# State products four in a row into banks of two rings, and a contiguous tap table written in two bursts

## The chip, the cores and the metric

The kernel runs on one core of one Trainium2 chip, alone. The core has four engines that compute, which run at the same time and wait for one another by semaphores: TensorE (PE in the profile, with its weight loads as PEld), VectorE (DVE), ScalarE (ACT) and GpSimd (POOL). SyncE (SP) issues the transfers (DMA). SBUF is the working memory of 128 partitions, PSUM the memory with banks into which PE writes, DRAM the large one outside the core. The metric is the device time of one execution in microseconds (us).

## The reference

Two layers over 1024 frames of 1024 channels. Layer 0 is an RWKV-7 mixer, layer 1 a diagonal state-space mixer of 64 groups with 16 channels and 64 complex states each; after each stands an MLP of 4096, and every part ends in a norm, x <- LayerNorm(alpha * x + f(x)). The change touches the second mixer alone:

```python
def s5_mix(x, a_re, a_im, log_dt, b_re, b_im, c_re, c_im, d_skip, w_glu):
    ...
    def chunk_step(h, u_c):
        h_re, h_im = h
        bu_re = jnp.einsum('tbgc,gpc->tbgp', u_c, bbar_re)
        bu_im = jnp.einsum('tbgc,gpc->tbgp', u_c, bbar_im)
        pr, pi, sr, si = lax.associative_scan(combine, (a_ch_re, a_ch_im, bu_re, bu_im), axis=0)
        carry_re, carry_im = cmul(pr, pi, h_re[None], h_im[None])
        s_re = sr + carry_re
        s_im = si + carry_im
        y = (jnp.einsum('tbgp,gcp->tbgc', s_re, cr_w)
             - jnp.einsum('tbgp,gcp->tbgc', s_im, ci_w))
        return (s_re[-1], s_im[-1]), y
    ...
    y = y.transpose(2, 0, 1, 3, 4).reshape(bsz, seq, d) + xf * d_skip.astype(f32)
    y = jax.nn.gelu(y).astype(x.dtype)
    z = y @ w_glu
    return z[..., :d] * jax.nn.sigmoid(z[..., d:])
```

## The kernel before

The 1024 frames are worked on as two halves A and B of 512, channels on the partitions, in eight blocks of 128 channels. While one half is in a mixer, the other runs its MLP, so that PE has dense work beside the mixer's small steps. A scheduler orders the instructions of each engine: each has a due number (`rank` sets it for a part), and of what is ready the lowest goes first. Tables have 99500, the state-space layer 99300 (half A) and 99400 (half B), norms 99000.

**Dense products.** A weight block of 128x512 comes by SP into `wraw` (2 buffers, L169), ACT casts it to `whi` (L148), DVE subtracts to get `wlo` (L149; 3 buffers each), and PE does three products for each pair of high and low parts into `d` (L188). A block is 12 matmuls.

**Tables** (`s5_tables`, about 1070 to 1270 us of the profile). For each block f of 8 groups: `bc` is loaded, DVE and POOL expand it to `ca` and `bp` (L1110 to L1138), `ca` goes to the table tC in DRAM. PE makes the taps `pk` (L1151): the answer of a group to an input 0 to 7 frames back, for 16 channels, the even groups of a pair on partitions 0 to 15, the odd ones on 64 to 79 ("par"). ACT copies them into `kpad` (L1155), whose front half was cleared once by POOL (L1106), so that shifted windows of it read zeros. Two transfers (L1159, one for each par) write eight shifted windows of it as the tap table tT[f], with the group g as the innermost axis. kpad has one buffer, so the next block's copy waits until both have been read. Then `bs` goes to tB (L1168).

**State-space stage** (`s5`, once for A and once for B). The inputs are turned to sub-chunks of 8 frames: `u1`, `ug`. L1206 makes the input to each chunk's state from `tb`, DVE and POOL run the scan over 64 chunks in `hb`. Then the outputs, in four turns f2 of two blocks each: the tables `tt` (from tT, L1240) and `tcm` (from tC, L1242) come in four buffers that they share with `tb`; for each par in turn PE sums in one bank of the ring pc (2 banks) the tap products (L1250, 128 contracted rows, 64 columns of `ug` as weights, 128 moving columns of `tt`) and the state products (L1255, 64 contracted rows). With j the block of the pair, the two j write the two halves of the bank's partitions. ACT copies the bank to `y1` (L1257). PE turns y1 block by block into `pyt` (L1263, a bank of the ring pa, 2 banks), DVE adds the skip term (`yg`, one buffer), ACT does the Gelu (L1267) and SP stores `s_y` (L1268); `yl` reads it back for the GLU that follows.

A 64x64 product takes one quadrant of PE's array. The order between taps and states within a turn is the scheduler's. The norms use the ring pl (one bank, "l"), `d` a ring of 3.

Of the kernel before, what the change touches and what calls it, by code (L numbers as in the profile page):

```python
# [30 lines left out]
LNG = (1, 3, 5)  # L31
LNT = (2, 5)
TB = 2
LN8R = 400000
MIXR = 100
W0B = 5
# [34 lines left out]
def trunk(ctx, tc, A):  # L71
# [90 lines left out]
    def wload(src, kt, n, key=None):  # L162

        step = 512 // n
        out = []
        for k0 in range(0, kt, step):
            kept = low.get((key, k0)) if key else None
            raw = wp.tile([128, step, n], F32, tag="wraw", name="wraw", bufs=2)
            SP.dma_start(raw, src[:, k0 : k0 + step])  # L169
# [12 lines left out]
        return out  # L182

    bulk, hops = [], []
    ST = getattr(nc, STE)
# [833 lines left out]

    SL = 8  # L1020
    NSC = HT // SL
    tT = dr.tile([KT, 128, 2, 512], F32, name="tT")
    tB = dr.tile([KT, 128, 4, 2, 128], F32, name="tB")
    tC = dr.tile([KT, 128, 4, 2, 128], F32, name="tC")

    def s5_tables():
# [75 lines left out]
        V.tensor_sub(ci, ci, tq)  # L1102
        V.tensor_mul(ci, ci, den)

        kpad = pp.tile([128, 16, 16, 4], F32, name="kpad")
        G.memset(kpad, 0.0)  # L1106
        for f in range(KT):
            gs = slice(4 * f, 4 * f + 4)
            bc = pp.tile([128, 2, 2, 4, 16], F32, tag="bc", name="bc", bufs=1)
            SP.dma_start(bc, A["s5bc"][f])  # L1110
            bb = pp.tile([128, 2, 4, 16], F32, tag="bb", name="bb", bufs=1)
# [40 lines left out]
                                  ca[ps_, g2, ri, 0:8].rearrange("p t c -> p (t c)"), start=ri == 0, stop=ri == 1)  # L1152
            for par in range(2):
                ps_ = slice(64 * par, 64 * par + 16)
                S.copy(kpad[ps_, 8:].rearrange("p t c g -> p g (t c)"), p[ps_])  # L1155
            tv = tT[f].rearrange("(s c) two n -> two c s n", c=16)
            for par in range(2):
                src = kpad[64 * par : 64 * par + 16, 1:9].rearrange("p t c g -> p (t c g)")
                SP.dma_start(tv[par], bass.AP(src.tensor, src.offset, [src.ap[0], (64, SL), src.ap[1]]))  # L1159

            bs = pp.tile([128, 4, 2, 128], F32, tag="bs", name="bs", bufs=1)
            for hf in range(2):
# [10 lines left out]
    def s5(H, h):  # L1173
# [61 lines left out]
        for f2 in range(4):  # L1235
            y1 = s5p.tile([128, SL, 4, 2, 16], F32, tag="u1", name="y1", bufs=2)
            tabs = []
            for f in (2 * f2, 2 * f2 + 1):
                tt = s5p.tile([128, 2, 512], F32, tag="tab", name="tt", bufs=4)
                SP.dma_start(tt, tT[f])  # L1240
                tcm = s5p.tile([128, 4, 2, 128], F32, tag="tab", name="tcm", bufs=4)
                SP.dma_start(tcm, tC[f])  # L1242
                tabs.append((f, tt.rearrange("p two (n g) -> p two g n", g=4), tcm))
            for par in range(2):
                qs = slice(64 * par, 64 * par + 64)
                p = pc.tile([128, HT], F32, tag="c", name="py").rearrange("p (g n) -> p g n", g=4)

                for g2 in range(4):
                    for j, (f, tv, tcm) in enumerate(tabs):
                        PE.matmul(p[64 * j : 64 * j + 64, g2], ug[f][:, 2 * g2 + par], tv[:, par, g2],  # L1250
                                  start=g2 == 0, stop=False, skip_group_check=True)
                for g2 in range(4):
                    for ri in range(2):
                        for j, (f, tv, tcm) in enumerate(tabs):
                            PE.matmul(p[64 * j : 64 * j + 64, g2], hb[qs, 4 * f + g2, ri, 0:NSC], tcm[qs, g2, ri],  # L1255
                                      start=False, stop=ri == 1, skip_group_check=True)
                S.copy(y1[:, :, :, par].rearrange("p t g c -> p g t c"), p.rearrange("p g (t c) -> p g t c", t=SL))  # L1257
            for j in range(2):
                f = 2 * f2 + j
                js = slice(64 * j, 64 * j + 64)  # L1260
                p = pa.tile([128, SL, NSC], F32, tag="a", name="pyt")
                for t in range(SL):
                    PE.transpose(p[:, t], y1[js, t].rearrange("p g r c -> p (g r c)"), ident[js, js])  # L1263
                y = s5p.tile([128, HT], F32, tag="yg", name="yg", bufs=1)
                V.scalar_tensor_tensor(y.rearrange("p (c t) -> p t c", t=SL), h[f].rearrange("p (c t) -> p t c", t=SL),
                                       vec("d", f), p, op0=ALU.mult, op1=ALU.add)
                S.activation(y, y, AF.Gelu_apprx_tanh)  # L1267
                SP.dma_start(scr["y"][f * 128 : (f + 1) * 128, H * HT : (H + 1) * HT], y)  # L1268
# [127 lines left out]
```

## Time and profile before

| | before |
|---|---|
| median of 3 runs | 2742.12 us (2735.79 to 2742.68) |
| profiled execution, its own time | 2746.6 us |
| span in the profile | 2744.8 us |
| granted TensorE clock, mean | 0.961 |
| ACT busy | 1154.8 us (42%) |
| POOL busy | 630.6 us (23%) |
| DMA moved | 345.90 MB, mean 126 GB/s |

The profile is of one execution, and its span leaves out 1.8 us around it. In the rows below, "x" is a count; for a tile the view gives the shortest, median and longest duration in ns, then the first and last start. A row of a timeline is start, length, engine, line, operation, out<-in, shape and count, and in brackets the idle time before it and what ended it. A row of waits is the engine and its line, what it waited for, then the sum in us, the times, and the longest. "SPq" is SP's queue of transfers. An fp32 matmul leaves two records.

### The profile page before, as it was taken

The numbers are of one execution on the slowest core, as the hardware profiler recorded it, in microseconds if no ns is written. First come the engines' busy times: TensorE is split into PE (matmuls) and PEld (weight loads), VectorE is DVE, ScalarE is ACT, GpSimd is POOL, SyncE is SP. The second block draws the span as 40 slices with busy tenths as digits, with TensorE's granted clock in tenths as the row PEclk, the third lists the DMA queues.
The fourth block names the chain that finished last, engine by engine and source line by source line (L and its number), as shares of the span: only waits on it lengthen the run. The fifth ranks groups of instructions, "written<-read, shape, count | busy, mean of one in ns | idle before, by whom it ended". The sixth has DMA issues, their size and how long they took to land.

```text
span 2744.8 us, 43807 instructions
## 1 busy us (share of the span) xinstructions
PE 2598.4 (95%) x16582; PEld 2089.9 (76%) x16582; DVE 1813.3 (66%) x3191; ACT 1154.8 (42%) x2038; POOL 630.6 (23%) x515
## 2 busy tenths in 40 slices
PE   7999979989899999989999999999999999999997
PEld 5778757678677777767876788778778887788886
DVE  7477677577786867997567553674855546755556
ACT  7455574544543333353532332434223324433334
POOL 3121542432442122342122000120220101210101
PEclk9989979999899999999999999999999999999998
DMA  4765455564223334545333533233343322333333
GB/s 146 235 214 175 151 164 156 178 203 142 81 86 88 93 92 148 141 129 163 100 112 127 174 95 100 81 96 112 103 164 110 96 96 81 119 96 96 96 96 100
DMA packets 215058, 345.90 MB, mean 126 GB/s; under 512 B 21184, under 2 KB 75584, under 8 KB 214848
## 3 DMA queue, kind: packets, MB, share of 16 engines
q1 hardware_dynamic: 214848, 343.10, 40.5%
q8 instruction: 131, 2.15, 0.3%
q14 instruction: 79, 0.65, 0.1%
HBM read 279.06 MB, written 63.96 MB: 125 GB/s over the span
## 4 chain that ended last, share of the span: by engine, by line
PE 44%; DVE 4%; issue 3%; DMA 1%; POOL 1%; ACT 1%; ACTq 0%; SPq 0%; DVEq 0%; POOLq 0%
PE d L188 39%; PE py L1250 1%; PE py L1255 1%; DVE wlo L149 1%; DMA wraw<-in_mw_dram 1%; PE pu L154 1%; PE pbu L1206 1%; POOL rl L975 1%; DVE hA L991 0%; DMA s_y<-yg 0%; DVE t L1218 0%; DVE hB L991 0%; ACT whi L148 0%; DVE sq L876 0%; PE pu L1195 0%
## 5 line engine op out<-in xcount | busy, mean ns | idle before, releaser
L148 ACT CAST whi<-wraw 128x512 fp32r<-128x512 f32 x668 | 413.5, 620 | 929.1 <-PE d L188 623.2
L149 DVE TENSOR_TENSOR wlo<-wraw,whi 128x512 fp32r<-128x512 f32 x668 | 500.6, 750 | 426.8 <-ACT whi L148 404.3
L188 PE MATMUL d<-qbuf,whi 128*128 128x512 f32 (+1 forms) x2112 | 657.0, 394 | 23.8 <-DVE hA L991 12.8
L188 PEld LDWEIGHTS d<-qbuf,whi 128*128 128x128 f32 x2112 | 391.8, 191 | 120.0 <-DVE hA L991 17.8
L188 PE MATMUL d<-qbuf,wlo 128*128 128x512 f32 (+1 forms) x1056 | 411.9, 392 | 10.7 <-DVE wlo L149 10.4
L975 POOL TENSOR_TENSOR rl<-rl 128x512 f32<-128x512 f32 x128 | 157.2, 1228 | 1094.5 <-ACT rl L974 1094.5
L188 PE MATMUL d<-oAh,whi 128*128 128x512 f32 (+1 forms) x960 | 390.9, 411 | 15.5 <-ACT ev L418 6.3
L188 PE MATMUL d<-oAl,whi 128*128 128x512 f32 (+1 forms) x960 | 387.5, 405 | 3.0 <-DVE oAl L149 2.8
L188 PE MATMUL d<-oAh,wlo 128*128 128x512 f32 (+1 forms) x960 | 386.5, 405 | 2.4 <-DVE wlo L149 2.3
L188 PE MATMUL d<-oBh,whi 128*128 128x512 f32 x704 | 279.2, 397 | 0.0
L188 PE MATMUL d<-oBh,wlo 128*128 128x512 f32 x704 | 278.7, 396 | 0.2 <-DVE wlo L149 0.2
L188 PE MATMUL d<-oBl,whi 128*128 128x512 f32 x704 | 277.1, 394 | 0.0
L188 PEld LDWEIGHTS d<-qbuf,wlo 128*128 128x128 f32 x1056 | 201.7, 191 | 56.5 <-DVE wlo L149 14.5
L188 PEld LDWEIGHTS d<-oAh,whi 128*128 128x128 f32 (+1 forms) x960 | 185.9, 194 | 62.2 <-ACT ev L418 8.4
L188 PEld LDWEIGHTS d<-oAh,wlo 128*128 128x128 f32 (+1 forms) x960 | 185.8, 194 | 44.4 <-DVE wlo L149 3.2
L188 PEld LDWEIGHTS d<-oAl,whi 128*128 128x128 f32 (+1 forms) x960 | 185.6, 194 | 43.1 <-DVE oAl L149 5.2
L991 DVE TENSOR_TENSOR hB<-hB,d 128x512 f32<-128x512 f32 (+1 forms) x256 | 165.0, 650 | 71.2 <-PE d L188 68.0
L991 DVE TENSOR_TENSOR hA<-hA,d 128x512 f32<-128x512 f32 x240 | 162.1, 682 | 64.4 <-PE d L188 62.1
L188 PEld LDWEIGHTS d<-oBh,wlo 128*128 128x128 f32 x704 | 132.9, 189 | 32.4 <-issue 2.0
L188 PEld LDWEIGHTS d<-oBl,whi 128*128 128x128 f32 x704 | 133.1, 189 | 29.9 <-issue 0.7
L188 PEld LDWEIGHTS d<-oBh,whi 128*128 128x128 f32 x704 | 133.1, 189 | 29.0 <-issue 1.2
L149 DVE TENSOR_TENSOR qbuf<-rl,qbuf 128x512 fp32r<-128x512 f32 x128 | 95.0, 742 | 73.5 <-ACT qbuf L148 73.5
(374 smaller groups left out, 3804.8 us busy)
## 6 DMA issues: line engine op xcount, KB each, us to landing
wraw<-in_mw_dram SPq DMA_DIRECT2D x520, 256.0 KB, 2.7
wraw<-in_glu_dram SPq DMA_DIRECT2D x64, 256.0 KB, 2.7
low<-wlo SPq DMA_DIRECT2D x52, 256.0 KB, 2.6
wlo<-low SPq DMA_DIRECT2D x52, 256.0 KB, 3.6
wraw<-in_wk_dram SPq DMA_DIRECT2D x32, 256.0 KB, 3.5
wraw<-in_wr_dram SPq DMA_DIRECT2D x32, 256.0 KB, 3.9
wraw<-in_wv_dram SPq DMA_DIRECT2D x32, 256.0 KB, 4.3
yl<-s_y SPq DMA_DIRECT2D x32, 256.0 KB, 3.1
```

The lines of the kernel that those rows point to most:

```text
L148: S.copy(hi, src)
L149: (e or V).tensor_sub(lo, src, hi.bitcast(F32))
L154: PE.matmul(out, x, idt, start=True, stop=True)
L188: bulk.append((PE.matmul(p, w, x, **kw).ins, x.shape[-1]))
L975: G.tensor_mul(r, r, r)
L991: V.tensor_add(z, z, p)
L1206: PE.matmul(p[qs, g2, ri], tb[:, g2, ri, qs], u[:, 2 * g2 + par], start=True, stop=True)
L1250: PE.matmul(p[64 * j : 64 * j + 64, g2], ug[f][:, 2 * g2 + par], tv[:, par, g2], start=g2 == 0, stop=False, skip_group_check=True)
L1255: PE.matmul(p[64 * j : 64 * j + 64, g2], hb[qs, 4 * f + g2, ri, 0:NSC], tcm[qs, g2, ri], start=False, stop=ri == 1, skip_group_check=True)
```

## The change

The taps keep their values; the table's layout, the order of products and the banks change.

```diff
+    def inorder(prods):
+        for x, y in zip(prods, prods[1:]):
+            tc.add_manual_dep(y.ins, x.ins.name, mybir.DependencyInfo(
+                mybir.DependencyClass.NoSync, mybir.DependencyReason.DATA), reason="order")
...
-    tT = dr.tile([KT, 128, 2, 512], F32, name="tT")
+    tT = dr.tile([128, 2, KT, 4, 128], F32, name="tT")
...
-        kpad = pp.tile([128, 16, 16, 4], F32, name="kpad")
-        G.memset(kpad, 0.0)
+        kpads = [pp.tile([128, TBF, 4, 16, 16], F32, name=f"kpad{j}") for j in range(KT // TBF)]
+        for kpad in kpads:
+            G.memset(kpad[:, :, :, 0:8], 0.0)
         for f in range(KT):
+            kpad = kpads[f // TBF]
...
-                S.copy(kpad[ps_, 8:].rearrange("p t c g -> p g (t c)"), p[ps_])
-            tv = tT[f].rearrange("(s c) two n -> two c s n", c=16)
-            for par in range(2):
-                src = kpad[64 * par : 64 * par + 16, 1:9].rearrange("p t c g -> p (t c g)")
-                SP.dma_start(tv[par], bass.AP(src.tensor, src.offset, [src.ap[0], (64, SL), src.ap[1]]))
+                S.copy(kpad[ps_, f % TBF, :, 8:].rearrange("p g t c -> p g (t c)"), p[ps_])
+            if f % TBF == TBF - 1:
+                for par in range(2):
+                    for s in range(SL):
+                        SP.dma_start(
+                            tT[16 * s : 16 * s + 16, par, f - TBF + 1 : f + 1].rearrange("c f g n -> c (f g) n"),
+                            kpad[64 * par : 64 * par + 16, :, :, 1 + s : 9 + s].rearrange("c f g t e -> c (f g) (t e)"))
...
-                SP.dma_start(tt, tT[f])
+                SP.dma_start(tt.rearrange("p two (g n) -> p two g n", g=4), tT[:, :, f])
-                tabs.append((f, tt.rearrange("p two (n g) -> p two g n", g=4), tcm))
+                tabs.append((f, tt.rearrange("p two (g n) -> p two g n", g=4), tcm))
+            pp = [r.tile([128, HT], F32, tag=t, name="py").rearrange("p (g n) -> p g n", g=4)
+                  for r, t in ((pc, "c"), (pa, "a"))]
+            for g2 in range(4):
+                for par in range(2):
+                    for j, (f, tv, tcm) in enumerate(tabs):
+                        PE.matmul(pp[par][64 * j : 64 * j + 64, g2], ug[f][:, 2 * g2 + par], tv[:, par, g2], ...)
+            prods = []
+            for g2 in range(4):
+                for ri in range(2):
+                    for j, (f, tv, tcm) in enumerate(tabs):
+                        for par in range(2):
+                            qs = slice(64 * par, 64 * par + 64)
+                            prods.append(PE.matmul(pp[par][64 * j : 64 * j + 64, g2], hb[qs, 4 * f + g2, ri, 0:NSC],
+                                                   tcm[qs, g2, ri], ...))
+            inorder(prods)
...
-                p = pa.tile([128, SL, NSC], F32, tag="a", name="pyt")
+                p = pl.tile([128, HT], F32, tag="l", name="pyt").rearrange("p (t n) -> p t n", t=SL)
```

So the even par of a turn sums in a bank of pc and the odd one in a bank of pa; the tap products of both come first, and the state products follow in a fixed order in which four neighbours lie on the four quadrants. TBF is 4.

On PE, at the end of turn f2 = 0 and in turn 1 of half A's outputs, there stood before (L1250 taps, L1255 states, L1263 transposes; counts are matmuls):

```order
L1250 MATMUL py<-tt,ug 64x128
L1263 MATMUL pyt<-ident,y_13883 128x64 x16
L1250 MATMUL py<-tt,ug 64x128 x7
L1255 MATMUL py<-tcm,hb 64x128 x16
L1250 MATMUL py<-tt,ug 64x128 x8
L1255 MATMUL py<-tcm,hb 64x128 x16
```

and 21 dense matmuls followed ahead of the next group. Now (L1262 taps, L1270 states, L1280 transposes, L195 dense) there stands:

```order
L1280 MATMUL pyt<-ident,y_13901 128x64 x8
L1262 MATMUL py<-tt,ug 64x128 x14
L1270 MATMUL py<-tcm,hb 64x128 x6
L1280 MATMUL pyt<-ident,y_13901 128x64 x8
L1270 MATMUL py<-tcm,hb 64x128 x26
L195 MATMUL d<-oBh,whi 128x512
L195 MATMUL d<-oBl,whi 128x512
L1262 MATMUL py<-tt,ug 64x128 x2
```

after which 20 dense matmuls follow. The first two taps of the next turn moved up behind the state products, and the second block's transposes into the middle of them.

On SP's queue, at the end of the tables, there stood before (tT L1159, tB L1168, tb L1200; `wraw` are weights):

```order
L1144 DMA tC<-ca 1024x1x128
L169 DMA wraw<-in_mw_dram 128x512 x2
L1159 DMA tT<-kpad 16x8x512 x2
L169 DMA wraw<-in_mw_dram 128x512
L1168 DMA tB<-bs 128x1024
L169 DMA wraw<-in_mw_dram 128x512
L1200 DMA tb<-tB 128x1024 x4
```

Now (tC L1153, tT L1168, tB L1179, tb L1211):

```order
L1153 DMA tC<-ca 1024x1x128
L170 DMA wraw<-in_mw_dram 128x512 x2
L1168 DMA tT<-kpad_12866 16x16x128 x16
L1179 DMA tB<-bs 128x1024
L170 DMA wraw<-in_mw_dram 128x512 x2
L1211 DMA tb<-tB 128x1024 x4
```

Sixteen writes stand where two stood, ahead of both last weight blocks; the other burst of sixteen stands after block f = 3, and the writes of the other blocks have left the places between the weights.

In half A's outputs SP's queue now runs (s_y is the store L1285, yl the read back L953):

```order
L170 DMA wraw<-in_mw_dram 128x512 x2
L1285 DMA s_y<-yg 128x512
L1251 DMA tt<-tT 128x2x512
L1253 DMA tcm<-tC 128x1024
L953 DMA yl<-s_y 128x512
L1285 DMA s_y<-yg 128x512
L1251 DMA tt<-tT 128x2x512
```

The first `tt` here is that of block f = 4, which stands behind the first s_y as it did before; its two first tap products have moved up on PE as shown above.

More of the change, by code (lines that the diff above doesn't have):

```diff
@@ L33 @@
 TB = 2
+TBF = 4
 LN8R = 400000
@@ new lines, in s5 @@
+                tabs.append((f, tt.rearrange("p two (g n) -> p two g n", g=4), tcm))
[4 more added lines that the diff above has]
+                    for j, (f, tv, tcm) in enumerate(tabs):
+                        PE.matmul(pp[par][64 * j : 64 * j + 64, g2], ug[f][:, 2 * g2 + par], tv[:, par, g2],
+                                  start=g2 == 0, stop=False, skip_group_check=True)
@@ L1258, in s5 @@
+            inorder(prods)
+            for par in range(2):
+                S.copy(y1[:, :, :, par].rearrange("p t g c -> p g t c"), pp[par].rearrange("p g (t c) -> p g t c", t=SL))
             for j in range(2):
```

13 lines of the change are left out of this document (1 added, 12 removed).

## The prediction

> **What bounds the kernel now.** I read the page's head first, then the windows by stage, because the average hides which engine sets which stage.
>
> ```profile
> span 2744.8 us, 43807 instructions
> PE 2598.4 (95%) x16582; PEld 2089.9 (76%) x16582; DVE 1813.3 (66%) x3191; ACT 1154.8 (42%) x2038; POOL 630.6 (23%) x515
> ```
>
> TensorE (PE) is busy 95% of the span, so time taken off PE counts wherever PE is what the stage waits for. The windows below (length; then busy time of PE, weight loads, DVE, ACT and POOL; granted clock; DMA share; GB/s) cover the first output stage of the state-space layer (1380 to 1545), the end of the second, and the stretch in which the tables are made (1150 to 1300):
>
> ```profile
> 1380.00:1420.00 40.00, 40.00 (x315) 31.49 (x315) 22.56 (x29) 12.82 (x22) 14.43 (x8) 1.00 0.43 136
> 1420.00:1480.00 60.00, 52.35 (x210) 39.80 (x209) 57.21 (x104) 15.86 (x27) 12.57 (x8) 0.96 0.25 77
> 1480.00:1545.00 65.00, 65.00 (x547) 49.40 (x546) 30.90 (x42) 23.02 (x38) 8.68 (x5) 0.99 0.64 219
> 2030.00:2075.00 45.00, 45.00 (x344) 34.13 (x343) 22.62 (x30) 16.05 (x28) 2.10 (x2) 1.00 0.53 186
> 1150.00:1180.00 30.00, 28.50 (x179) 21.05 (x177) 29.46 (x44) 11.38 (x16) 13.30 (x10) 1.00 0.73 184
> 1180.00:1210.00 30.00, 22.73 (x115) 16.93 (x112) 29.65 (x40) 12.80 (x21) 13.04 (x10) 0.86 0.48 128
> 1268.00:1300.00 32.00, 31.33 (x140) 25.54 (x139) 20.42 (x34) 9.89 (x17) 3.60 (x3) 1.00 0.61 188
> ```
>
> Both output stages show PE busy without a gap (65.00 of 65.00, 45.00 of 45.00), so what their small products lose, the span loses. Between them and the first tap products lies a stretch that DVE sets (57.21 of 60), and the tables are made first under DVE (29.65 of 30), then under PE (31.33 of 32).
>
> **The small products, and what becomes shorter.** An fp32 matmul stands as two records. The tile view of py gives counts (weight loads have rows of their own), the timeline of PE the pace:
>
> ```profile
> L1255 PE MATMUL py<-tcm,hb x512: 269/269/473, 1481.2 to 2057.2; 64*64 64x128 f32 x171
> L1250 PE MATMUL py<-tt,ug x256: 388/406/422, 1401.4 to 2055.1; 128*64 128x128 f32 x128
> 1399.47 2.08 PE L1206 MATMUL pbu<-ug,tb 128*64 128x64 f32 x64
> 1401.39 1.07 PE L1250 MATMUL py<-tt,ug 128*64 128x128 f32 x4
> 1402.39 0.50 PE L188 MATMUL d<-oBh,whi 128*128 128x512 f32 x1
> 1490.55 2.01 PE L1250 MATMUL py<-tt,ug 128*64 128x128 f32 x14
> 1492.49 1.96 PE L1255 MATMUL py<-tcm,hb 64*64 64x128 f32 x32
> 1494.38 2.01 PE L1250 MATMUL py<-tt,ug 128*64 128x128 f32 x16
> 1407.86 3.84 PE L1250 MATMUL py<-tt,ug 128*64 128x128 f32 x28
> 1481.22 3.55 PE L1255 MATMUL py<-tcm,hb 64*64 64x128 f32 x64
> ```
>
> A group's length ends with one record's whole pass, so the pace is (length - pass)/(count - 1). State products (L1255): (3.55 - 0.27)/63 = 52 ns; with the changes of tile shape at the ends of a group of 32, 54.5 ns. Tap products (L1250): (3.84 - 0.41)/27 = 127 ns in this one group and (2.01 - 0.41)/15 = 107 in another; I take 114.
>
> Tap products: the moving operand is read at every fourth element. L1206 has the same 128*64 tiles, half the columns and a contiguous operand, at (2.08 - 0.22)/63 = 29.5 ns a record; 128 columns would take 59, and the state products with 128 columns take 54.5. I take 54.6 for a contiguous tap record: 256 x (114 - 54.6) = **15.2 us** gone. If stride is not the cause, nothing goes.
>
> State products: today two tiles are in flight, the two column halves of one row half. Where the first par's last products overlapped the second's first ones, the trace shows what four tiles do (windows of L1255 alone):
>
> ```profile
> 1482.00:1482.30 0.30, 0.30 (x10) 0.30 (x8) 1.00 0.95 362
> 1482.90:1483.20 0.30, 0.30 (x18) 0.30 (x16) 1.00 0.20 48
> 1483.50:1483.80 0.30, 0.30 (x10) 0.30 (x8) 1.00 0.93 335
> ```
>
> In 0.3 us stood 18 records instead of 10, counting those still in flight. The forced order makes that the whole of them: 512 x (54.5 - 27.3) = **13.9 us** gone. L1206's pace of 29.5 ns with a 64-column weight load for each record speaks for it, since loads do not limit there. [...]
>
> Together 29.1 us, 14.6 a stage. It counts nearly whole: the stages have no idle PE, and the first taps, ahead of the stretch that DVE sets, hold DVE up too (waits from 1400 to 1420):
>
> ```profile
> DVE wlo L149 <- PE d L188: 5.4, 1, 5.4
> ```
>
> DVE stood 5.4 us behind PE there, more than the 32 records (1.9 us) save.
>
> **What the output stage gives back.** Two tap matmuls of the next turn now stand right behind the state products, with 0 to 2 dense matmuls between where there were 18 to 21. They need tt of block 4 (then 6), which is released by the tap products of the turn ahead and stands on SP's queue behind the store s_y. In the trace s_y leaves at 1492.21, and a tt takes about 4 us:
>
> ```profile
> 1498.22 0.51 PE L188 MATMUL d<-oBh,whi 128*128 128x512 f32 x1
> 1492.21 0.33 SPq L1268 DMA_DIRECT2D s_y<-yg  x1
> 1496.42 0.32 SPq L1240 DMA_DIRECT2D tt<-tT  x1
> DMA to landing us min/median/max: 3.8/4.2/6.2
> ```
>
> Landing thus at about 1496.5, wanted at about 1494.5 (that turn's state products gave way to the dense product at 1498.22; a turn now saves 14.6/4 = 3.7 us): a **stall of 2 us**, twice a stage, 8 us in both stages. Bounds 0 (s_y leaves 2 us sooner because its turn's products are quicker) and 14 us. Changes of tile shape: 16 taps took 1494.38 to the next start at 1496.33, 1.95 us, 0.13 more than 16 x 0.114; the lone group of 4 took 1.0 us, from 1401.39 to 1402.39, against 4 x 0.114 = 0.46. So a pair put alone costs 0.13 to 0.54 us, three turns a stage, and the transposes now cut in two add one change a turn: I take 1 us a stage, **2 in all**, bounds 0 and 4. The turned outputs in the norm bank wait at most for one another; DVE, half idle (30.90 of 65), hides that.
>
> **The table writes.** Before, every block f wrote two transfers of 256 KB; now, twice, after four blocks, sixteen of 128 KB, in a row on SP's queue ahead of weights that used to stand between. What matters is their rate. Windows in which only such a transfer ran (16 partitions), and one in which tC ran (128 partitions, the same 512-byte packets as the new ones):
>
> ```profile
> 1191.50:1193.50 2.00, 2.00 (x13) 1.67 (x12) 2.00 (x4) 1.95 (x5) 2.00 (x3) 1.00 0.93 104
> 1221.40:1223.40 2.00, 2.00 (x10) 1.66 (x9) 2.00 (x5) 1.97 (x4) 0.52 (x1) 1.00 0.92 102
> 1153.60:1155.00 1.40, 1.40 (x8) 1.13 (x6) 1.40 (x3) 0.00 (x0) 0.55 (x1) 1.00 1.04 325
> ```
>
> A transfer from 16 partitions runs at 104 GB/s with the DMA engines 93% busy; one from 128 at 325. The new ones still come from 16 partitions (first eight all from the lower 16, then eight from the upper), so a burst of 2.1 MB takes 2.1/0.104 = **20 us**; at the other rate it would be 6.5. The second burst falls here (DMA issues, then ACT and PE):
>
> ```profile
> 1268.48 0.86 SPq L1159 DMA_DIRECT2D tT<-kpad  x2
> 1270.90 0.42 SPq L169 DMA_DIRECT2D wraw<-in_mw_dram  x1
> 1277.22 2.07 SPq L1200 DMA_DIRECT2D tb<-tB  x4
> 1275.71 0.62 ACT L148 CAST whi<-wraw 128x512 fp32r<-128x512 f32 x1 [2.19 <-PE d L188]
> 1286.53 1.25 ACT L148 CAST whi<-wraw 128x512 fp32r<-128x512 f32 x2 [7.72 <-PE d L188]
> 1287.20 1.19 PE L188 MATMUL d<-qbuf,whi 128*128 128x512 f32 x4 [0.67 <-ACT whi L148]
> ```
>
> The weight block issued at 1270.90 would land at about 1268.5 + 2 + 20 = 1291 instead of by 1275.7. With three whi buffers PE reaches it two blocks of 12 x 0.228 = 2.74 us after the cast, at 1281; it would start at 1292: **11 us** of idle PE. The block behind the four tb transfers, ready at 1287 with 0.7 us of PE idle today, waits perhaps 1 us more. I take **12**, bounds 1 (6.5 us burst) and 17 (nothing behind it buffered). The first burst, near 1172, delays weights and bc by the same 20 us, but there DVE sets the pace (29.65 of 30 busy), in part with norms and table products that need no new weights. No row prices that; I take it that all but a fifth of the 20 us is covered: **4**, bounds 0 and 8.
>
> What goes: SP's waits at the old writes and the single buffer behind them (waits of SP's queue, 1120 to 1275), and POOL's clearing doubles:
>
> ```profile
> SPq L1159 <- ACT kpad L1155: 12.4, 8, 4.5
> L1106 POOL MEMSET kpad<- x1: 965/965/965, 1072.4 to 1072.4; 128x1024 f32 x1
> ```
>
> Fourteen of the sixteen places where weights stood behind a waiting write are gone; under DVE's pace I give it **-1** (0 to -3). Clearing goes from 0.97 to about 4 x 0.97 us, by elements; POOL is under half busy and the longest norm step waits for it once: **+0.5** (0 to 3). The contiguous copy on ACT and tt's shorter packets cost nothing: ACT is 42% busy, and tt's landing is priced above.
>
> **Sum**, against the profiled execution of 2746.6 us (span 2744.8): -29.1 + 8 + 2 + 12 + 4 - 1 + 0.5 = **-3.6**, so 2743. The median of the runs, 2742.1, lies 4.5 us below the profiled one; from it the forecast is **2738 us**.
>
> **The rivals.**
> *The bursts are hidden.* If packets of 512 bytes go at tC's 325 GB/s, the two bursts cost 1 + 0.5 instead of 16: -3.6 - 14.5 = -18, 2724. The 104 GB/s rows speak against it, since only the partitions are alike in both; but the packet's size does change.
> *The tap loads come late* (slower). A tt stands behind s_y, which stands behind a transpose, DVE and a Gelu, with one yg buffer. If each of these takes 4 us longer than I read, four such stalls grow from 2 to 6 us: +16, so +12, 2754. It decides from about 3 us more a turn (-3.6 + 4 x 3 = +8). For it: PE has less dense work between turns to cover a late s_y. Against: s_y's own inputs come sooner by 2 to 4 us.
> [...]
>
> **Chances.** Forecast 0.57, bursts hidden 0.20, late taps 0.15, no gain in one of the products 0.08. A measurement here can tell about 0.3%, 8.2 us, from no change. The forecast's own bounds (4 to 8 us either way in the stalls) put 0.13 of its 0.57 beyond -8.2 and 0.09 beyond +8.2; hidden bursts are faster whole; late taps 0.14 slower; the last 0.06 slower. Faster 0.33, same 0.38, slower 0.29. The range takes in hidden bursts and late taps: 2722 to 2756.
>
> **What would show it.** In the changed profile: tap records at 55 ns and state records at 27 ns in the timeline; tT windows at 104 GB/s (forecast) or over 300 (hidden bursts); PE idle about 11 us before the first dense products after the second burst; PE idle 2 us on tt behind each turn's state products, twice a stage. If the output stages win less than 5 us each, or PE never stalls near 1281 to 1292, the forecast is wrong at that step.

## The result, and the profile after

The changed kernel takes 2755.93 us (median of 8 runs, 2751.20 to 2761.17), the kernel before 2738.16 us beside it (8 runs, 2726.34 to 2749.15). The ratio is 1.0062, with a 95% interval of 1.0044 to 1.008: **slower by some 17 us**, where 4 us less was forecast. The head of the page of the changed kernel:

```profile
span 2753.8 us, 43799 instructions
PE 2568.3 (93%) x16582; PEld 2071.4 (75%) x16582; DVE 1819.2 (66%) x3191; ACT 1143.5 (42%) x2038; POOL 632.0 (23%) x516
```

PE's busy time fell by 30.1 us (2598.4 to 2568.3), and yet the span grew by 9.0. So about 39 us of idle time are new. Two places have most of them. One caution first: the last start of these transposes, ahead of everything that the change touches (the tile view of py, kernel before and after):

```profile
L778 PE MATMUL py<-ident,o x64: 270/272/454, 298.0 to 1068.5; 128*128 128x128 f32 x64
L785 PE MATMUL py<-ident,o x64: 270/273/472, 295.8 to 1061.3; 128*128 128x128 f32 x64
```

The first 1068 us, which do the same in both, ran 7.2 us quicker in this one execution. Counted from there the changed kernel loses 9.0 + 7.2 = 16 us, which agrees with the timed 17. Below, times are therefore differences inside a stage, not positions. PE's busy time holds some of this too: up to there it is 983.2 us before and 977.6 after. So 5.6 of the 30.1 us have nothing to do with the change, and that 30.1 lies so near to the 29.1 forecast for the products is in part luck.

From there to the first output stage (kernel before, then after: length, PE busy, granted clock, DMA share, GB/s):

```profile
1068.50:1478.34 409.84, 381.41 (x2118) 0.97 0.45 131
1061.30:1491.99 430.69, 381.07 (x2124) 0.95 0.43 125
```

This stretch, with the tables in it, is 20.9 us longer, all of it idle time of PE. The two output stages win back only 3.8 us.

**The tables.** SP's issues around the second burst, then ACT and PE (timelines of the changed kernel):

```profile
1265.35 19.68 SPq L1168 DMA_DIRECT2D tT<-kpad  x16
1285.13 1.39 SPq L1179 DMA_DIRECT2D tB<-bs  x1
1286.62 2.76 SPq L170 DMA_DIRECT2D wraw<-in_mw_dram  x2
1292.48 0.65 DVE L998 TENSOR_TENSOR hA<-hA,d 128x512 f32<-128x512 f32 x1 [16.41 <-DMA wraw<-in_mw_dram]
1292.64 1.23 ACT L149 CAST whi<-wraw 128x512 fp32r<-128x512 f32 x2 [22.16 <-DVE hb L1187]
1293.31 2.07 PE L195 MATMUL d<-qbuf,whi 128*128 128x512 f32 x4 [15.25 <-ACT whi L149]
```

The sixteen writes hold SP's queue for 19.68 us. The next weight is cast 27.3 us after the burst's start, and PE stands 15.25 us. ACT's row names a step of DVE, but DVE's own row at that place shows what both waited for, the landing of the weight. The first burst makes an idle time of PE of 9.95 us in the same way, and DVE stands too, because the next block's `bc` is behind the writes (timelines of PE and DVE):

```profile
1192.19 0.79 PE L195 MATMUL d<-oAh,whi 128*128 128x512 f32 x1 [9.95 <-ACT whi L149]
1190.73 0.23 DVE L1125 TENSOR_TENSOR bb<-bc,q 128x64 f32<-128x64 f32 x1 [7.93 <-DMA bc<-in_s5bc_dram]
```

From 1061 to the first output stage PE waits 27.0 us for `whi`; before it was 1.8. Windows over the second burst (rate in the last column), and behind it (granted clock third from the end):

```profile
1266.00:1284.00 18.00, 12.06 (x55) 9.60 (x54) 5.96 (x9) 3.26 (x6) 1.04 (x1) 0.98 0.75 106
1284.00:1288.00 4.00, 0.00 (x0) 0.00 (x0) 0.00 (x0) 0.00 (x0) 0.00 (x0) 0.50 0.79 93
1292.00:1296.00 4.00, 2.69 (x6) 2.15 (x7) 2.54 (x5) 1.23 (x2) 0.00 (x0) 0.50 0.78 276
```

The rate is close to the forecast 104 GB/s, and in the second window all engines that compute are empty. PE also comes back at a clock of 0.50.

**The output stages.** Windows from the cast of one weight block to that of another, the same blocks in both kernels (blocks 317 to 335 in the first stage, 476 to 493 in the second; length, PE busy, clock, DMA share, GB/s), before and after:

```profile
1478.34:1564.47 86.13, 86.01 (x633) 0.98 0.56 190
2004.92:2088.04 83.12, 82.87 (x614) 0.96 0.49 165
```

```profile
1491.99:1573.73 81.74, 74.76 (x628) 0.96 0.60 200
2014.69:2098.40 83.71, 73.16 (x610) 0.94 0.51 167
```

PE has 21 us less to do in them (168.88 to 147.92), but the stages are only 3.8 us shorter (169.25 to 165.45): 17.5 us of PE idle time where there was 0.4. The timeline of PE names what it waited for, after the groups that show the new pace:

```profile
1505.62 1.96 PE L1262 MATMUL py<-tt,ug 128*64 128x128 f32 x28
1508.73 1.75 PE L1270 MATMUL py<-tcm,hb 64*64 64x128 f32 x52
1512.80 0.65 PE L1262 MATMUL py<-tt,ug 128*64 128x128 f32 x4 [1.65 <-DMA tt<-tT]
1525.67 0.65 PE L1262 MATMUL py<-tt,ug 128*64 128x128 f32 x4 [1.84 <-DMA tt<-tT]
1544.58 0.68 PE L1280 MATMUL pyt<-ident,y 64*128 64x64 f32 x8 [2.85 <-DVE hb L1189]
```

Taps run at (1.96 - 0.27)/27 = 63 ns a record instead of 114, states at (1.75 - 0.27)/51 = 29 ns instead of 54.5. Then PE waits for tt as forecast, and for something that was not. The last row's wait ends when DVE has finished the yg step ahead of L1189 (timeline of DVE):

```profile
1543.31 1.13 DVE L1282 SCALAR_TENSOR_TENSOR yg<-hA,pv,pyt 128x512 f32<-128x512 f32 x1 [4.53 <-DMA s_y<-yg]
```

The one bank of the norms holds the first block's turned outputs until DVE may write the single yg, which waits for the store before it. In both windows together PE waits 8.8 us for tt, 3.0 us for DVE's step on turned outputs and 2.0 us for ACT's copy of the sums (rows of waits); the rest of the idle time is in smaller waits.

That wait is also followed by a lower clock (windows of PE behind it):

```profile
1545.00:1546.00 1.00, 1.00 (x9) 1.00 0.30 117
1547.00:1548.00 1.00, 1.00 (x4) 0.50 0.54 182
```

PE is at work again, and yet its granted clock is 0.50 in the second of these windows; from 1550 to 1551 it is 1.00 again. Dense records start every 0.43 us in the stretch at 0.50 (1546.69 to 1549.25 in the timeline of PE) and every 0.23 us at 1.00 (1537.92 to 1541.34). The mean clock in the two output stages is 0.96 and 0.94, where it was 0.98 and 0.96, so the 21 us somewhat understate what the products save.

### The profile page after: what moved, and what is told of

It is laid out like the page before. It is cut to its first block, busy times and chain, and to the rows that moved or that the text cites. A ratio compares the mean times of both kernels' runs of the same rounds, so it can differ in the third digit from the quotient of the medians.

```text
span 2753.8 us, 43799 instructions
## 1 busy us (share of the span) xinstructions
PE 2568.3 (93%) x16582; PEld 2071.4 (75%) x16582; DVE 1819.2 (66%) x3191; ACT 1143.5 (42%) x2038; POOL 632.0 (23%) x516
## 4 chain that ended last, share of the span: by engine, by line
PE 56%; DVE 15%; DMA 6%; issue 5%; ACT 3%; POOL 2%; SPq 2%; ACTq 0%; DVEq 0%; POOLq 0%
PE d L195 49%; DVE wlo L150 3%; DMA wraw<-in_mw_dram 2%; DMA s_y<-yg 1%; SPq L1168 1%; PE pA L603 1%; ACT whi L149 1%; DMA yl<-s_y 1%; POOL rl L982 1%; DVE hA L998 1%; PE pbu L1217 1%; PE pu L155 1%; DVE xh L648 1%; DVE qbuf L150 1%; DVE x L646 1%
## 5 line engine op out<-in xcount | busy, mean ns | idle before, releaser
L195 PE MATMUL d<-qbuf,whi 128*128 128x512 f32 (+1 forms) x2112 | 656.5, 394 | 45.6 <-ACT whi L149 16.3
L195 PEld LDWEIGHTS d<-qbuf,whi 128*128 128x128 f32 x2112 | 391.3, 191 | 141.8 <-DVE hA L998 22.9
L195 PE MATMUL d<-oAh,whi 128*128 128x512 f32 (+1 forms) x960 | 392.2, 412 | 28.3 <-ACT whi L149 9.9
L195 PE MATMUL d<-qbuf,wlo 128*128 128x512 f32 (+1 forms) x1056 | 410.6, 391 | 6.8 <-DVE wlo L150 6.7
L982 POOL TENSOR_TENSOR rl<-rl 128x512 f32<-128x512 f32 x128 | 154.6, 1208 | 1076.7 <-ACT rl L981 1069.2
L195 PE MATMUL d<-oAl,whi 128*128 128x512 f32 (+1 forms) x960 | 387.5, 405 | 1.3 <-DVE oAl L150 1.3
L195 PE MATMUL d<-oAh,wlo 128*128 128x512 f32 (+1 forms) x960 | 386.9, 405 | 1.5 <-DVE wlo L150 1.5
L195 PE MATMUL d<-oBh,whi 128*128 128x512 f32 x704 | 278.8, 396 | 0.7 <-ACT whi L149 0.7
L195 PE MATMUL d<-oBh,wlo 128*128 128x512 f32 x704 | 278.5, 396 | 0.2 <-DVE wlo L150 0.2
L195 PE MATMUL d<-oBl,whi 128*128 128x512 f32 x704 | 277.0, 394 | 0.0
L195 PEld LDWEIGHTS d<-oAh,whi 128*128 128x128 f32 (+1 forms) x960 | 186.1, 194 | 73.9 <-ACT whi L149 11.3
L195 PEld LDWEIGHTS d<-qbuf,wlo 128*128 128x128 f32 x1056 | 201.0, 191 | 52.9 <-DVE wlo L150 10.8
L195 PEld LDWEIGHTS d<-oAh,wlo 128*128 128x128 f32 (+1 forms) x960 | 185.6, 194 | 43.8 <-DVE wlo L150 3.0
L195 PEld LDWEIGHTS d<-oAl,whi 128*128 128x128 f32 (+1 forms) x960 | 186.5, 194 | 40.9 <-DVE oAl L150 2.6
L195 PEld LDWEIGHTS d<-oBh,wlo 128*128 128x128 f32 x704 | 132.5, 188 | 32.9 <-issue 2.0
L195 PEld LDWEIGHTS d<-oBl,whi 128*128 128x128 f32 x704 | 132.7, 188 | 30.3 <-issue 1.3
L195 PEld LDWEIGHTS d<-oBh,whi 128*128 128x128 f32 x704 | 132.8, 189 | 29.4 <-ACT whi L149 1.6
```

What stands on the lines that cost most here:

```text
L195: bulk.append((PE.matmul(p, w, x, **kw).ins, x.shape[-1]))
L982: G.tensor_mul(r, r, r)
```

## The experiments

Each ratio is to the kernel before, run on the same chip, with its 95% interval; the experiments ran on several chips, so they are compared by their ratios. Lengths of the output stages are those of the two windows above, added: 169.2 us before, 165.4 after.

### The parts alone

The table part alone (kernel before, with kpad in two buffers, two bursts, contiguous taps):

```diff
-    tT = dr.tile([KT, 128, 2, 512], F32, name="tT")
+    tT = dr.tile([128, 2, KT, 4, 128], F32, name="tT")
...
+            if f % TBF == TBF - 1:
+                for par in range(2):
+                    for s in range(SL):
+                        SP.dma_start(...)
```

> The kernel before with the table part alone: two padded buffers, two bursts of sixteen writes, contiguous taps; order and banks of the outputs as before. Theory A (the bursts hold SP's queue for about 20 us each and cost 21 to 23 us, the outputs win only a little): tap records at 62 ns save about 12 us, so 9 to 11 us slower than before. Theory B (the loss is in the output stages, by the late tap loads and the norms' bank, and the bursts cost little): about 10 us faster than before.

Ratio 1.006 (1.0037 to 1.0084), about 16 us slower. The loss of the whole change is here: theory B falls. Theory A named the place, but asked for 9 to 11 us. SP was held for 19.10 and 19.19 us, and PE stood 13.72 us behind the second burst.

The output part alone:

```diff
-                p = pc.tile([128, HT], F32, tag="c", name="py")...
+            pp = [r.tile([128, HT], F32, tag=t, name="py")... for r, t in ((pc, "c"), (pa, "a"))]
...
+            inorder(prods)
...
-                p = pa.tile([128, SL, NSC], F32, tag="a", name="pyt")
+                p = pl.tile([128, HT], F32, tag="l", name="pyt")...
```

> The kernel before with the output part alone: state products four in a row, odd bank from the other ring, turned outputs in the norms' bank; table, its writes and the stride of the taps as before. Theory A: state products save 14 us, stalls on tt and on the norms' bank take back about 11, so 2 to 4 us faster than before. Theory B: 10 or more us slower than before.

Ratio 1.001 (0.9996 to 1.0025): nothing gained, though state products alone were to bring 13.9 us. The output stages take 167.6 us, of which PE idles 13.6. Theory B falls here too, and theory A's gain of 2 to 4 us did not come.

### The bursts

The changed kernel with the table written block by block again; so that two transfers of 2 KB runs do it and the taps stay contiguous in runs of 16, the table's order is frame, group, channel:

```diff
-        kpads = [...]
+        kpad = pp.tile([128, 16, 4, 16], F32, name="kpad")
...
+            tv = tT[f].rearrange("(s c) two n -> two c s n", c=16)
+            for par in range(2):
+                src = kpad[64 * par : 64 * par + 16, 1:9].rearrange("p t g c -> p (t g c)")
+                SP.dma_start(tv[par], bass.AP(src.tensor, src.offset, [src.ap[0], (64, SL), src.ap[1]]))
```

> The changed kernel with the tap table written block by block as before (two transfers of 16x8x512 for each block, one padded buffer), with runs of 16 channels contiguous in it. Theory A: PE's idle time near 1185 and 1290 goes, 21 to 23 us less than the changed kernel, so about 4 us faster than before. Theory B: as the changed kernel, 15 to 17 us slower than before. If runs of 16 do not count as contiguous, taps keep 114 ns, and it comes out some 13 us above theory A's time.

Ratio 0.9972 (0.9957 to 0.9988), about 8 us faster than before, 25 us below the changed kernel. Taps keep their short records (273 ns median, 28 of them in 1.96 us, both as in the changed kernel), so runs of 16 are long enough.

The changed kernel with the writes of a burst by turns from the lower and the upper partitions:

```diff
-                for par in range(2):
-                    for s in range(SL):
+                for s in range(SL):
+                    for par in range(2):
```

> The changed kernel with the sixteen writes of a burst in another order: lower and upper partitions by turns instead of eight of the one and then eight of the other; bytes, packets and places as in the changed kernel. Theory A (a transfer from 16 partitions is limited by them, and two from different partitions run beside each other): the rate in a burst goes from about 100 to about 200 GB/s, SP is held about 10 us instead of 19.7, PE's idle time of 15.3 us at the second burst falls to about 5, and the whole is 10 to 14 us less than the changed kernel. Theory C (the 512-byte packets or the issues on SP's queue set the rate): rate and time as in the changed kernel.

Ratio 1.0008 (0.9996 to 1.0019), some 15 us less than the changed kernel, by the order of two loops. SP, and PE behind the second burst:

```profile
1264.04 13.58 SPq L1168 DMA_DIRECT2D tT<-kpad  x16
1283.58 2.07 PE L195 MATMUL d<-qbuf,whi 128*128 128x512 f32 x4 [6.83 <-ACT whi L149]
```

Same bytes, packets and issues, 13.6 us instead of 19.7, and 6.8 us of idle PE instead of 15.3. So theory C falls: with the same packets, the order of the partitions in the queue takes the rate from 93 to 112 GB/s in the changed kernel's second burst to 138 to 179 here, the direction that theory A named. Its size came only in part, since the rate did not reach 200 GB/s (windows inside the second burst):

```profile
1266.00:1272.00 6.00, 6.00 (x30) 4.96 (x29) 4.37 (x7) 1.95 (x4) 1.04 (x1) 1.00 0.76 138
1272.00:1276.00 4.00, 4.00 (x19) 3.30 (x19) 1.41 (x3) 0.00 (x0) 0.00 (x0) 1.00 0.82 179
```

### What takes the output stages' gain

Three experiments each take one named wait away. The turned outputs in the ring pa, in the changed kernel (`pl.tile(..., tag="l")` to `pa.tile(..., tag="a")`):

> The changed kernel with the turned outputs back in the ring pa of two banks. Theory A: PE's waits of 2.9, 2.0 and 0.2 us for the norms' bank go, 3 to 5 us less than the changed kernel, still 11 to 14 us slower than before. Theory B: 10 us or more less than the changed kernel. A third reading (the odd sums now fill pa, so that ring of two is no better than one bank): no change.

Ratio 1.0102 (1.0078 to 1.0127): not less than the changed kernel but more. The wait of PE for tt in the second stage went from 4.9 to 9.1 us (rows of waits, changed kernel, then this one):

```profile
PE py L1262 <- DMA tt<-tT: 4.9, 3, 2.7
PE py L1262 <- DMA tt<-tT: 9.1, 4, 3.4
```

All three readings missed: PE's waits for the turned outputs went, as theory A said, but the output stages grew to 169.8 us, and none of the three forecast a loss. Its profiled execution, 2756.52 us, is the quickest of its six runs (median 2767.88), so the trace cannot explain the whole size, which stays open.

On e3_perblock, the store issued by ACT, then the turned outputs in two banks, then both:

```diff
-                SP.dma_start(scr["y"][...], y)
+                S.dma_start(scr["y"][...], y)
...
-                p = pl.tile([128, HT], F32, tag="l", name="pyt")...
+                p = (pa if j else pl).tile([128, HT], F32, tag="a" if j else "l", name="pyt")...
```

> The kernel e3_perblock with the store s_y issued by ACT right behind the Gelu instead of by SP, so that tt no longer stands behind it on SP's queue. Theory A2 (tt comes late because it stands behind s_y): PE's waits on tt, 7.3 us in both output stages of e3_perblock, fall to under 2, and the whole is 4 to 7 us less than e3_perblock. Theory D (tt is late because its buffer comes free late and it takes 4 us): waits as in e3_perblock, no change of time.

> The kernel e3_perblock with the turned outputs in two banks: the first block of a turn in the norms' bank, the second in the ring pa. Theory A3 (the single bank, held by DVE's step until the store of the block ahead has landed, makes PE wait): PE's waits for pyt, 6.3 us in both stages of e3_perblock, go to under 2 us, and the whole is 3 to 5 us less. Theory E (as with pa alone in e4_pyt_pa, the waits only move to tt): no change or some us more.

> e6_store_act and e7_pyt_two together, on e3_perblock. If A2 and A3 hold, PE's idle time in the output stages from 1470 on falls by about 10 us, and the whole is 7 to 11 us less than e3_perblock, some 15 us or 0.6% less than the kernel before; under D and E it is as e3_perblock.

Ratios 1.0005 (0.9989 to 1.0021), 0.9979 (0.9965 to 0.9993), 0.9999 (0.9987 to 1.0012), against 0.9972 of e3_perblock. None is better, and the output stages are longer in all three: 172.9, 168.0 and 169.9 us, against 162.5. The waits move, as E said. In e7_pyt_two those for tt go from 7.4 to 16.2 us. In e6_store_act those for tt stay at 7.1, so that A2 falls, and those for ACT's copy of the sums rise from 0.8 to 6.7. Next, the contiguous taps without anything else (the kernel before with e3_perblock's edit to kpad and its order), and yg in two buffers (in the norms' scratch) on e3_perblock and on that kernel:

```diff
-                y = s5p.tile([128, HT], F32, tag="yg", name="yg", bufs=1)
+                y = tp.tile([128, HT], F32, tag="la", name="yg", bufs=2)
```

> The kernel before with nothing but contiguous taps: the table's order is frame, group, channel, written block by block as before; order of the products, banks and stride of all else as before. Theory F (in the output stages only the contiguous taps are worth something; four in a row and the other banks give back what they save): as fast as e3_perblock or faster, 8 to 12 us less than the kernel before. Theory G (both parts save, and their savings add up in e3_perblock): only 3 to 6 us less than before.

> The kernel e3_perblock with yg in two buffers (the ring of the norms' scratch) instead of one. Theory H (with quicker products the stage is set by the chain of each block, transposes, DVE, Gelu, store, landing, next block's DVE, with its single yg): DVE's waits on the landing of s_y, 16 us in e3_perblock, go, PE's waits for pyt fall from 6 to under 2 us, and the whole is 4 to 8 us less than e3_perblock. Rival (the waits move to tt, as they did in e7_pyt_two): no change of time.

> e9_taps_only with yg in two buffers. Theory H: where PE is slower the chain hides, so within 2 us of e9_taps_only. Rival (the chain sets the stage in both): 4 us or more less than e9_taps_only.

e9_taps_only 0.9966 (0.9951 to 0.9981), as fast as e3_perblock: theory F. Four in a row with the new banks is worth nothing. The second yg buffer alone is worth nothing either (0.9986, 0.9967 to 1.0006; 0.9972, 0.9954 to 0.9991): theory H falls as a single cause (DVE's waits on the landing went, but PE's on tt rose from 7.4 to 10.0 us). Then four in a row with the banks of before, on e9_taps_only (the lines are against e3_perblock, from which it differs by these alone):

```diff
-                  for r, t in ((pc, "c"), (pa, "a"))]
+                  for r, t in ((pc, "c"), (pc, "c"))]
...
-                p = pl.tile([128, HT], F32, tag="l", name="pyt")...
+                p = pa.tile([128, SL, NSC], F32, tag="a", name="pyt")
```

> e9_taps_only with the state products four in a row, but in the banks of before: both sums of a turn in the two banks of pc, the turned outputs in pa. The next turn's taps then find no free bank until ACT has copied one, and stand behind about 20 dense products as before. Theory I (the waits of the changed output stages come from the bank choice, which lets the next taps and the transposes move up ahead of what feeds them): PE's idle time in the two output stages stays at about 4 us as in e9_taps_only, state records run at 27 ns, and the whole is 8 to 13 us less than e9_taps_only, about 20 us or 0.8% less than before. Theory J (whatever the banks, the chain of stores and loads sets the stage once PE is quicker): 14 us of idle time comes back, and it is as e9_taps_only.

Ratio 0.9997 (0.9979 to 1.0015): theory I falls. The windows of the output stages, e9_taps_only and e12_states_pc:

```profile
1473.40:1554.63 81.23, 78.79 (x633) 0.99 0.60 202
1996.85:2073.95 77.10, 75.81 (x616) 0.98 0.53 178
```

```profile
1472.90:1554.60 81.70, 73.84 (x633) 0.93 0.60 201
1996.85:2076.31 79.46, 69.23 (x614) 0.94 0.51 173
```

PE is busy 11.5 us less, and idle 18.1 us instead of 3.7. So theory J's 14 us of idle time came back: whatever the banks, it fills what the quick products leave. By time this kernel is also some 8 us slower than e9_taps_only, where J forecast no difference; its windows show 2.8 us of that.

### Which link

The tap loads left out, the taps multiplying tcm instead; then with two yg buffers, with the store from ACT, and, as a control, without four in a row:

```diff
-                SP.dma_start(tt, tT[f])
-                tabs.append((f, tt.rearrange("p two (t g c) -> p two g t c", g=4, c=16), tcm))
+                tabs.append((f, tcm.rearrange("p g two n -> p two g n"), tcm))
```

> e12_states_pc with the tap table not read: the tap products take tcm as their moving operand, in the same shape, count and order, so the tap loads are left out and tcm has all four buffers, a turn ahead. Theory K (the landing of the tap loads is the link): PE's 18 us of idle time in the two output stages falls to under 9, and the whole is 8 us or more less than e12_states_pc. Theory L (the chain of each block's store is the link): the waits move to pyt and idle time stays at 14 to 18 us, time within 3 us of e12_states_pc.

> e13_no_tt with yg in two buffers; the tap loads are left out as there. Theory K: within 3 us of e13_no_tt. Theory L: idle time falls by 5 us or more against e13_no_tt. If both links count, only this one and the next come near the 4 us of idle time of e9_taps_only.

> e13_no_tt with the store s_y issued by ACT behind the Gelu; the tap loads are left out as there. Theory K: within 3 us of e13_no_tt. Theory L with the store's issue on SP's queue as the slow step: idle time falls by 5 us or more against e13_no_tt.

> The control: e9_taps_only (order and banks of before) with the tap loads left out in the same way. Under both theories the loads are hidden behind the slower products there, so the time is within 3 us of e9_taps_only; if it is 6 us or more less, tap loads cost more than the waits named after them show, and e13_no_tt has to be read against this one.

Ratios 0.996 (0.9943 to 0.9978), 0.9952 (0.9934 to 0.997), 0.9953 (0.9936 to 0.9971) and 0.9979 (0.9963 to 0.9995). The two output stages in the traces, with the two kernels of the next step (us; the waits are those that the rows of waits name for PE):

| kernel | length | PE idle | PE waits for tt | for ACT's copy of the sums |
|---|---|---|---|---|
| before | 169.2 | 0.4 | 0 | 0 |
| after | 165.4 | 17.5 | 8.8 | 2.0 |
| e9_taps_only | 158.3 | 3.7 | 2.5 | 0 |
| e12_states_pc | 161.2 | 18.1 | 7.7 | 6.2 |
| e13_no_tt | 161.9 | 17.9 | 0 | 14.8 |
| e14_no_tt_yg_two | 156.6 | 12.6 | 0 | 12.4 |
| e15_no_tt_act | 154.5 | 14.0 | 0 | 13.8 |
| e16_no_tt_old | 161.5 | 2.8 | 0 | 2.8 |
| e17_pool_cast | 156.4 | 13.1 | 6.8 | 0.8 |
| e18_pool_yg_two | 148.2 | 9.9 | 8.4 | 0 |

Time and trace disagree on e13_no_tt. By its ratio it is about 10 us quicker than e12_states_pc, and the two kernels behind it lie within 3 us of it, all as K wants. In its one trace the stages are no shorter: the waits for tt are gone, and as much is waited for ACT's copy instead, as L wants. With two yg buffers idle time falls by 5.3 us, with the store from ACT by 3.9, where L asked for 5. So K isn't refuted as a part of the cause; that it is the whole cause does not fit the trace, and where e13_no_tt wins its 10 us stays open. In the control (e16_no_tt_old) nothing is gained against e9_taps_only. What PE waits for in e13_no_tt, and ACT's timeline at that place:

```profile
1525.99 1.60 PE L1274 MATMUL pyt<-ident,y 64*128 64x64 f32 x16 [5.16 <-ACT y L1268]
1522.83 0.63 ACT L1278 ACTIVATE yg<-yg 128x512 f32<-128x512 f32 x1 [3.30 <-DVE yg L1276]
1524.35 0.62 ACT L149 CAST oAh<-yl 128x512 fp32r<-128x512 f32 x1 [0.89 <-DMA yl<-s_y]
1524.87 1.07 ACT L1268 COPY y<-py 128x512 f32<-128x512 f32 x2
```

PE waits for ACT's copy of the finished sums, and that copy stands on ACT's queue behind a Gelu that waits for DVE (which waits for a store) and behind a cast that waits for the read-back yl. So the last two runs clear ACT's queue, on e12_states_pc with its tap loads: the split of yl for the GLU goes to POOL (its subtraction leaves DVE with it), then yg has two buffers as well.

```diff
+            if pool:
+                hi, lo = optile(H, "h"), optile(H, "l")
+                G.tensor_copy(hi, y)
+                G.tensor_sub(lo, y, hi.bitcast(F32))
...
-                y = s5p.tile([128, HT], F32, tag="yg", name="yg", bufs=1)
+                y = tp.tile([128, HT], F32, tag="la", name="yg", bufs=2)
```

> e12_states_pc with the two steps that split the read-back yl for the GLU (a cast on ACT, a subtraction on DVE) made by POOL instead. Theory M (ACT's copy of the sums is late because it stands behind the cast that waits for yl's landing): ACT's copies come right behind the state products, PE's 18 us of idle time in the two output stages falls by 6 us or more, and the whole is 4 to 8 us less than e12_states_pc. Theory K (tap loads): no change within 3 us.

> e17_pool_cast with yg in two buffers. Theory M with both links (the cast of yl and the Gelu that waits for the store): idle time falls to about 6 us, and the whole is 8 to 12 us less than e12_states_pc, about 1% less than before. Theory K: no change within 3 us; the taps still wait for tt.

Ratios 0.9956 (0.9939 to 0.9972) and **0.9929** (0.9908 to 0.995), so 11 and 18 us less than e12_states_pc by time. In e17_pool_cast idle time is 5 us less than there, where theory M asked for 6, and PE's waits for ACT's copy go from 6.2 to 0.8 us; in e18_pool_yg_two they are gone. So theory M's mechanism holds, with both links; whether the step taken off DVE adds to it was not run apart. The windows of e18_pool_yg_two:

```profile
1473.63:1549.75 76.12, 71.03 (x633) 0.97 0.63 215
1990.49:2062.58 72.09, 67.25 (x614) 0.96 0.59 191
```

The stages take 148.2 us, 21 less than before and 13 less than e12_states_pc. The clock was higher too: PE does the same products as in e12_states_pc in 4.8 us less (138.3 against 143.1), at a granted clock of 0.97 and 0.96 instead of 0.93 and 0.94. Idle are 9.9 us, where about 6 were expected: one wait for tt in each stage, 3.78 and 4.14 us, is most of it. That of the first:

```profile
1497.60 3.16 PE L1264 MATMUL py<-tt,ug 128*64 128x128 f32 x30 [3.78 <-DMA tt<-tT]
```

This kernel (contiguous taps written block by block, four in a row in the banks of before, POOL's split, two yg buffers; 2723.40 us, 6 runs, beside 2743.96) beats the kernel before by 0.7% and, ratio against ratio, the changed kernel by about 1.3%. POOL's split and two yg buffers were not run without four in a row. But PE's products alone take 154.6 us in the stages of e9_taps_only (78.79 + 75.81), so without four in a row the stages could hardly come down to 148.2.

## Why the prediction was wrong, point by point

Of the forecast -3.6 us, the output stages were to bring -29.1 + 8 + 2 = -19 and the tables +15.5. The traces show -3.8 in the two windows and +20.9 in the stretch ahead of them. So the larger miss is in the output stages.

- **What bounds the stages** was right: PE had 0.4 us of idle time in them. **The savings of the products** were right in size. Stride was the cause of the slow taps (e9_taps_only, where of the products it alone changed: records of 273 ns median instead of 406), and state products with neighbours on four quadrants do come at nearly twice the pace; the records come every 63 and 29 ns, where 54.6 and 27.3 were taken. In the windows PE's busy time fell by 21.0 us in the changed kernel, at a mean clock of 0.96 and 0.94, and by 30.6 us in e18_pool_yg_two, at 0.97 and 0.96. That one of the products gains nothing, 0.08 in the chances, falls by the same 63 and 29 ns.
- **It counts nearly whole**: this step failed. "The stages have no idle PE" is true of before, but the copies of ACT, the stores and the loads stood just hidden behind the slow products. With PE 21 us quicker in the two windows, they came late: 17.5 us of idle time, where 8 + 2 were allowed for. The stalls on tt were sized well (1.65 + 1.84 + 0.43 us in the first stage and 4.9 in the second, by the rows of waits, 8.8 in all against 8). The 2 us for changes of tile shape were not measured apart.
- **The norms' bank at nothing**: failed. DVE "half idle" says nothing of a bank that is held until a store has landed; PE's waits for DVE's step came to 3.0 us, 2.85 of them at 1544.58. Taking them away (e4, e7) showed that this was one of several waits of like length, none of which pays alone.
- **The second burst** was the right mechanism, mis-sized: 12 us forecast; measured 15.25 us of idle PE and 1.10 at 1301, against 0.67 before. PE ran out of weights 12.7 us after the burst's start, as forecast. But the working took the weight as landed 22.5 us after it, and it was cast at 27.3. It left out that SP issues the next weight only behind the sixteenth write and tB, 19.68 + 1.39 us, and that the weight was cast 6 us after its issue.
- **The first burst** at 4 us: failed. That DVE's pace covers it was wrong, because the writes also held back `bc`, on which DVE itself stood 7.93 us; PE stood 9.95. What both bursts cost in time is seen against the table written block by block: 25 us (e3), where 16 were forecast. The order of two loops alone takes 15 of them back (e5).
- **The clock** has no term in the sum. Behind the second burst and behind the wait at 1544.58 it was 0.50 while PE worked.
- **The small terms.** SP's waits at the writes fell from 13.8 to 1.2 us, and clearing on POOL took 3.65 us instead of 0.97, close to the 3.9 expected. No run prices either.
- **The rivals.** Hidden bursts fell by the rate of 106 GB/s. "The tap loads come late" named the right stage and the wrong link: it asked for four stalls of 6 us on tt, 24 in all, and 8.8 came; moving the store off SP's queue left 7.1 of 7.4 us (e6). That 2755.93 us still lies inside the range, at its upper end, is luck: it is the sum of misses in two places, and not the late taps for which the range was drawn that wide.

## What to carry to other kernels

An engine without idle time in a stage can hide chains that are just shorter (here 0.4 us of idle time before, 17.5 after). Before counting a saving there whole, go through the period of each loop (copy, step, store, single buffer) and the order of work on each engine in it, and ask which is next; here it was a PSUM copy on ACT behind steps that wait for a store's read-back (6.2 us of PE's waits in e12_states_pc, 0.8 in e17_pool_cast), and in the output stages' traces taking one wait away mostly handed the time to the next one until ACT's queue was cleared. Waits for tt are what is left there (8.4 us).

Many transfers gathered into a burst on a queue that also brings the weights cost what the buffered weights do not cover: here, with the weights two blocks ahead, 15.25 us of idle PE for a burst of 19.68. If a burst must be, alternate the partitions it reads; here that made it 13.58 us and left 6.83.

## What the runs showed of the hardware

- A transfer from 16 partitions runs at 102 to 104 GB/s alone (kernel before, 1221.4 to 1223.4 and 1191.5 to 1193.5, DMA engines shown as 92 to 93% busy), one from 128 partitions at 325 (1153.6 to 1155.0). In the second burst of the changed kernel the rate is 93 to 112 (74 to 79%); transfers from partitions 0 to 15 and 64 to 79 by turns reach 138 to 179 GB/s (e5_interleaved). The two sets did not reach twice the rate of one here.
- PE had no work from 1278.1 to 1293.3 us of the changed kernel's trace, and its granted clock was 0.50 from 1284 on, and still 0.50 up to 1296, in the window in which it began again. After the wait of 2.85 us that ended at 1544.58 it was 1.00 from 1545 to 1546 and 0.50 from 1547 to 1548.
- A moving operand with runs of 16 elements is read at the pace of a contiguous one (273 ns records, 28 in 1.96 us, in e3_perblock and in the changed kernel). One of every fourth element gives 406 ns records (kernel before), which come every 107 to 127 ns instead of every 63.
- Records of state products came every 54.5 ns in the kernel before, with neighbours on two quadrants, and every 29 ns in the changed kernel, with neighbours on four.
